# The eight value products of a pair of heads, recorded as one unbroken alternating run on TensorE

## The chip, the cores and the metric

One core of a Trainium2 chip runs the whole kernel. The metric is the device time of one execution in microseconds; a profile of one execution goes with it. The engines are TensorE (PE in the views; PEld for its weight loads), VectorE (DVE), ScalarE (ACT), GpSimd (POOL) and SyncE (SP), which issues most transfers.

## The reference

Two layers of a decoder trunk over 512 positions of width 1024. A layer projects its normed input once, runs three causal token mixers of eight heads of 64 on it, gates each, projects each back, merges and adds. Cut to what matters here:

```python
for l in range(DEPTH):                        # 2 layers
    z = u @ w_in                              # one projection for all mixers
    ya = dsa_attention(...)                   # a: softmax over the top 128 keys of an indexer
    yb = swa_sinks_attention(...)             # b: softmax over a window of 128, with sinks
    yc = stick_breaking_attention(...)        # c: stick-breaking weights, no softmax
    # each of them ends with the value product of every head, for example
    #   einsum('bhts,bshd->bthd', a, v)       # weights (512 x 512, causal) times values (512 x 64)
    merged = sum(sigmoid(m) * ((y * silu(g)) @ w_br) for y, g, m, w_br in ...)
    x = x + gate * (merged @ w_out)
```

## The kernel before

Everything lies transposed: features on the 128 partitions, the 512 positions along the free axis. Weights come from HBM in chunks `wstage` and are split into a high part `whi` and a low part `wlo`; activations are split in the same way (`uh` and `ul`, and both halves of a tile `Y`). A wide projection of one output tile `ps_z` is then 24 matmuls of 512 columns: eight slices of the input with three products each.

A mixer works on pairs of heads, four pairs (0 to 3) each, in the order c, b, a. For a pair, `c_qk` or `softmax_qk` makes the weights in tiles `t` (products `KH,Q` and `klow,Q`), `softmax_tr` transposes them in blocks of 128 on TensorE (`small,t`) and copies them back to tiles `t`, and `softmax_pv` multiplies them with the values `vc`, `vb` or `va`. This last step is the one that changes. The two heads of a pair share one PSUM tile `y` (a `ps_s`): head 0 has partitions 0 to 63, head 1 has 64 to 127. Each head has four products, one for each block j of 128 keys. In mixers a and c they are 512, 384, 256 and 128 columns wide, in mixer b 256, 256, 256 and 128. They are in float32, and each of them leaves two records in the profile. The first product of a head (j is 0) opens its half of the bank, the others add to it. `finish_pair` then multiplies `y` with the gate (`e<-ps_s,G`), and splits it into the two halves of `Y`, which the branch products (`ps_z<-Y,whi` and `ps_z<-Y,wlo`) read.

No operation is issued where it is written. `Weave` first puts the streams of one layer (indexer, top-k search, mixers, projections) into one sequence. Each operation is then recorded by `Recorder.add`, which finds what it depends on, and priced by `Recorder.price`. A list scheduler, `Recorder.forward`, gives every engine its order from these prices and from priorities of earlier rounds, and `Recorder.emit` issues that order. The scheduler may put any other ready TensorE operation between two recorded ones. An operation named `pairs` is an exception: it is recorded once, holds a list of matmuls, and `emit` issues them back to back. Before the change only `low_parts` uses it, for products `klow,Q` of 64 rows. In the views line 553 is where `emit` issues such a list, and line 555 where it issues everything else.

The value products are recorded one by one, the heads in turn for each j:

```python
for j in range(4):
    for e in range(2):
        ...
        mm(y[64 * e:64 * e + 64, 128 * j:128 * j + W], st["v" + b][:, j, c:c + 64], PT[bk][:, c0:c0 + W], j == 0)
```

`price` knows them by their 64 columns of values, and gives each half of the time of its columns and 0.03 us.

Of the kernel before, what the change touches and what calls it, by code (L numbers as in the profile page):

```python
# [25 lines left out]
F32 = mybir.dt.float32  # L26
# [127 lines left out]
class View:  # L154
# [30 lines left out]
    def real(self):  # L185
        ap = self.tile.real()
        for name, arg, *more in self.ops:
            ap = ap.rearrange(arg, a=more[0]) if more else getattr(ap, name)(arg)
        return ap
# [60 lines left out]
class Recorder:  # L250
# [29 lines left out]
    def add(self, ways):  # L280
        x = Instr()
        x.i = len(self.list)
        op, args, kw = next(iter(ways.values()))
        if op == "pairs":
            named = [(("out", "in", "in")[n], v) for q in args for n, v in enumerate(q)]
        else:
            named = [("out" if "out" not in kw and n == 0 else n, v) for n, v in enumerate(args)] + list(kw.items())
        x.writes = [v for n, v in named if isinstance(v, View) and n in ("out", "accum_out")]
        x.reads = [v for n, v in named if isinstance(v, View) and n not in ("out", "accum_out")]
        x.preds, x.succs = {}, []  # L290
        for views, w in ((x.reads, False), (x.writes, True)):
            for v, r in [(v, r) for v in views for r in v.regions()]:
                t = v.tile
                if op == "matmul" and w and kw["start"]:
                    r = (r[0], r[1], 0, S)
                keep = []
                for (j, r2, w2) in t.seen:
                    over = r[0] < r2[1] and r2[0] < r[1] and r[2] < r2[3] and r2[2] < r[3]
                    if over and j is not x and (w or w2):
                        x.preds[j.i] = j  # L300
                    if not (w and over and r[0] <= r2[0] and r2[1] <= r[1] and r[2] <= r2[2] and r2[3] <= r[3] and j is not x):
                        keep.append((j, r2, w2))
                t.seen = keep + [(x, r, w)]
        x.tiles = list({id(v.tile): v.tile for v in x.reads + x.writes if not v.tile.pool.fixed}.values())
        for j in x.preds.values():
            j.succs.append(x)
        x.alts = {}
        for e, (op, args, kw) in ways.items():
            x.alts[e] = self.price(x, e, op, args, kw)
        x.prio = x.i  # L310
        self.list.append(x)

    def price(self, x, engine, op, args, kw):

        y = Way()
        y.op, y.args, y.kw, y.mode, y.port = op, args, kw, None, False
        o = x.writes[0] if x.writes else None
        if op == "preload_act_table_set":
            y.cost = y.lag = 1.3
            return y  # L320
        if op == "dma_start":
            n = 1
            for d in (o or x.reads[0]).shape:
                n *= d
            y.cost, y.lag, y.mode = 0.35 if engine == "SP" else 0.1, n * 4 / 365e3, "dma"
            return y
        n = 1
        for d in o.shape[1:]:
            n *= d
        from_psum = any(v.tile.pool.name[:3] == "ps_" for v in x.reads)  # L330
        if engine == "PE":
            if op == "pairs":
                w = [q[2].shape[-1] for q in args]
                c, y.mode = 0.095 + sum(max(0.112, 0.4375e-3 * v + 0.007) for v in w[::2]), "r"
                y.cost, y.lag = c, c + self.PIPE
            elif op == "transpose":
                c, y.mode = 0.109, "t"
                y.cost, y.lag = c, c + self.PIPE
            elif args[1].shape[-1] == 64:
                c, y.mode = 4 * n / 2.4e3 / 2 + 0.03, "c"  # L340
                y.cost, y.lag = c, 2 * c + self.PIPE
            else:
                rhs, y.mode = args[2], "m"
                c = 4 * n / 2.4e3 + 0.01 if rhs.dtype == F32 else 0.06 if rhs.dtype == BF16 else 0.4375e-3 * n + 0.007
                y.cost, y.lag = c, c + self.PIPE
            return y
        accum = "accum_out" in kw
        if engine == "ACT":
            b = 0.1 if isinstance(kw.get("bias"), View) or isinstance(kw.get("scale"), View) else 0.0
            c = 0.2 + 0.82e-3 * n + (b if not accum else 0.08) - (0.03 if from_psum else 0)  # L350
        elif engine == "DVE":
            y.port = not from_psum and op not in ("max", "match_replace", "memset", "reciprocal")
            if op == "tensor_tensor_scan":
                c = 1.21
            elif op == "max":
                c = 0.15 + 1.05e-3 * args[1].shape[-1]
            elif op == "match_replace":
                c = 0.145 + 1.05e-3 * args[2].shape[-1]
            elif n <= 16:
                c = 0.2 + (0.1 if accum else 0)  # L360
            elif op == "tensor_tensor_reduce":
                c = 0.147 + 1.05e-3 * n
            elif from_psum:
                c = 0.147 + 1.05e-3 * n + (0.08 if accum else 0)
            elif op in ("tensor_scalar", "tensor_copy"):
                c = 0.2 + 0.45e-3 * n if op == "tensor_scalar" else 0.15 + 0.5e-3 * n
            elif op == "memset":
                c = 0.1 + 0.6e-3 * n
            else:
                c = 0.15 + 1.05e-3 * n + (0.08 if accum else 0)  # L370
        else:
            y.port = n > 16
            if op == "memset":
                c = 0.12 if n < 16 else 0.52
            elif op == "tensor_copy":
                c = 0.2 + 0.82e-3 * n
            elif op == "tensor_scalar":
                c = 0.2 + 2.8e-3 * n
            else:
                c = 0.1 + 2.35e-3 * n  # L380
        y.cost = y.lag = c
        return y
# [162 lines left out]
    def emit(self, order):  # L545
        def real(v):
            return v.real() if isinstance(v, View) else v
        with self.tc.manual_schedule():
            for x, engine in order:
                y = x.alts[engine]  # L550
                if y.op == "pairs":
                    for q in y.args:
                        self.real[engine].matmul(*[real(a) for a in q], start=False, stop=True, skip_group_check=True)  # L553
                    continue
                getattr(self.real[engine], y.op)(*[real(a) for a in y.args], **{k: real(v) for k, v in y.kw.items()})  # L555

# [21 lines left out]
def trunk(ctx, tc, xT, vecs, w_ss, w_gt, w_first, w_t, w_v, w_br, w_o, rope, consts, out):  # L578
# [18 lines left out]
    def ybank():  # L597
        return rec.tile("ps_s", [P, S])
# [4 lines left out]
    def mm(o, lhsT, rhs, start, stop=True):  # L603
        PE.matmul(o, lhsT, rhs, start=start, stop=stop, skip_group_check=True)

    def pairs(quads):

        rec.add({"PE": ("pairs", tuple(quads), {})})
# [94 lines left out]
    st = {}  # L703
# [333 lines left out]
    def hold_topk(y):  # L1037

        POOL.tensor_copy(out=m8_tile()[:, 0:1], in_=f(y[:, 0:1]))
# [33 lines left out]
    def low_parts(q, kl, pos, banks, b, order):  # L1073

        quads = []
        for e, i in order:
            k0, W = keys(b, i)
            bk, c0 = pos(e, i)
            hp = (H0, H1)[e]
            quads.append((banks[bk][:, c0:c0 + W], q[hp, e, 128 * i:128 * i + 128], kl[hp, k0:k0 + W]))  # L1080
        pairs(quads)

    LOW_ALL = ((0, 3), (1, 3), (0, 2), (1, 2), (0, 1), (1, 0), (0, 0))
# [62 lines left out]
    def keys(b, i):  # L1146
        return (0, 128 * (i + 1)) if b != "b" else (max(0, 128 * (i - 1)), 256 if i else 128)
# [96 lines left out]
    def softmax_pv(b, p):  # L1244
        def fn():
            y = ybank()
            PT = st.pop(("pt", p))
            tpos = btpos if b == "b" else cpos
            for j in range(4):
                W = min(256, S - 128 * j) if b == "b" else S - 128 * j  # L1250
                for e in range(2):
                    bk, c0 = tpos(e, j)
                    h = 2 * p + e
                    c = 64 * (h // 4 if b == "b" else h)
                    mm(y[64 * e:64 * e + 64, 128 * j:128 * j + W], st["v" + b][:, j, c:c + 64], PT[bk][:, c0:c0 + W], j == 0)
            finish_pair(b, p, y)
            if b == "c":
                hold_topk(st["yc", p][0])
        return op(1500 if b == "b" else 2200, fn)
# [275 lines left out]
    for fn, chunks in wv.items:  # L1535
# [4 lines left out]
        args = [ch.get(pos - len(chunks) + i) for i in range(len(chunks))]  # L1540
# [65 lines left out]
```

## Time and profile before

| | |
|---|---|
| time, median of 3 runs | 1219.87 us (1219.51 to 1220.11) |
| profiled execution, first to last instruction | 1217.8 us; the page gives no other time of its own for it |
| TensorE busy | 1200.4 us (99%), 6006 records |
| VectorE busy | 962.1 us (79%) |
| ScalarE busy | 556.3 us (46%) |
| GpSimd busy | 264.3 us (22%) |
| moved by DMA | 139.40 MB, mean 114 GB/s |

A record of a matmul starts where the matmul starts; its end is modelled and lies under the next one. The time between the starts of two neighbours is therefore what a matmul takes of TensorE. The granted clock of TensorE is 0.998 of full speed over the span. Nearly all instructions carry the line of `emit`, so groups are told apart by the names of their tiles.

### The profile page before, as it was taken

The numbers are of one execution on the slowest core, as the hardware profiler recorded it, in microseconds if no ns is written. First come the engines' busy times: TensorE is split into PE (matmuls) and PEld (weight loads), VectorE is DVE, ScalarE is ACT, GpSimd is POOL, SyncE is SP. The second block draws the span as 40 slices with busy tenths as digits, with TensorE's granted clock in tenths as the row PEclk, the third lists the DMA queues.
The fourth block names the chain that finished last, engine by engine and source line by source line (L and its number), as shares of the span: only waits on it lengthen the run. The fifth ranks groups of instructions, "written<-read, shape, count | busy, mean of one in ns | idle before, by whom it ended". The sixth has DMA issues, their size and how long they took to land.

```text
span 1217.8 us, 17816 instructions
## 1 busy us (share of the span) xinstructions
PE 1200.4 (99%) x6006; PEld 976.3 (80%) x6006; DVE 962.1 (79%) x2106; ACT 556.3 (46%) x1166; POOL 264.3 (22%) x290
## 2 busy tenths in 40 slices
PE   9999999999999999999999999999999999999997
PEld 8899777788777887688898987777878878877886
DVE  6867999899879888686476699989996887667754
ACT  6623677454445532632143157664534654234222
POOL 1200446432111110011200015454220110100120
PEclk9999999999999999999999999999999999999999
DMA  9644222344334455245533432223442324323343
GB/s 318 231 119 124 83 70 84 104 114 117 109 96 122 129 146 150 69 130 145 171 109 98 133 95 78 85 69 116 121 122 70 96 80 120 95 64 79 93 123 102
DMA packets 81915, 139.40 MB, mean 114 GB/s; under 512 B 10016, under 2 KB 22560, under 8 KB 81824
## 3 DMA queue, kind: packets, MB, share of 16 engines
q1 hardware_dynamic: 80672, 136.17, 38.6%
q10 hardware_dynamic: 1152, 2.10, 0.5%
q8 instruction: 47, 0.77, 0.3%
q14 instruction: 44, 0.36, 0.1%
HBM read 125.39 MB, written 4.19 MB: 106 GB/s over the span
## 4 chain that ended last, share of the span: by engine, by line
PE 89%; DVE 4%; SPq 2%; DMA 2%; ACT 1%; issue 1%; POOL 1%; DVEq 0%; ACTq 0%; POOLq 0%
PE ps_z L555 67%; PE ps_s L555 22%; SPq L555 2%; PE ps_s L553 1%; DMA m<-zs 1%; DVE t L555 1%; DVE Q L555 1%; DVE m L555 1%; DMA wstage<-in_w_first 1%; DMA wstage<-in_w_t 0%; ACT t L555 0%; POOL KH L555 0%; DVE score L555 0%; DVE zc L555 0%; DVE den L555 0%
## 5 line engine op out<-in xcount | busy, mean ns | idle before, releaser
L555 PE MATMUL ps_z<-uh,whi 128*128 128x512 f32 (+1 forms) x908 | 359.1, 397 | 2.2 <-DVE xm L555 2.2
L555 PE MATMUL ps_z<-uh,wlo 128*128 128x512 f32 (+1 forms) x908 | 356.0, 393 | 0.0
L555 PE MATMUL ps_z<-ul,whi 128*128 128x512 f32 (+1 forms) x908 | 355.8, 392 | 0.0
L555 POOL TENSOR_TENSOR wlo<-wstage,whi 128x512 fp32r<-128x512 f32 (+1 forms) x131 | 175.1, 1339 | 662.8 <-DVE whi L555 312.0
L555 PEld LDWEIGHTS ps_z<-uh,whi 128*128 128x128 f32 x908 | 170.3, 188 | 41.9 <-DVE xm L555 3.1
L555 PEld LDWEIGHTS ps_z<-uh,wlo 128*128 128x128 f32 x908 | 170.5, 188 | 38.7 <-issue 1.8
L555 PEld LDWEIGHTS ps_z<-ul,whi 128*128 128x128 f32 x908 | 170.6, 188 | 35.9 <-issue 1.0
L555 DVE TENSOR_TENSOR wlo<-wstage,whi 128x512 fp32r<-128x512 f32 (+2 forms) x241 | 158.2, 660 | 12.8 <-ACT whi L555 3.6
L555 DVE CAST whi<-wstage 128x512 fp32r<-128x512 f32 (+2 forms) x181 | 74.7, 412 | 112.9 <-PE ps_z L555 94.5
L555 ACT CAST whi<-wstage 128x512 fp32r<-128x512 f32 (+2 forms) x141 | 83.4, 596 | 169.7 <-PE ps_z L555 125.9
L555 PE MATMUL ps_z<-Y,whi 128*128 128x512 f32 x384 | 121.7, 396 | 0.0
L555 ACT ACTIVATE e<-ps_z 128x512 f32<-128x512 f32 x68 | 40.2, 592 | 131.7 <-PE ps_z L555 131.4
L555 PEld LDWEIGHTS ps_z<-Y,whi 128*128 128x128 f32 x384 | 71.7, 188 | 17.0
L555 ACT ACTIVATE e<-e 128x512 f32<-128x512 f32 x96 | 60.6, 633 | 39.9 <-DVE e L555 39.1
L555 PE MATMUL ps_z<-Y,wlo 128*128 128x512 f32 x192 | 75.8, 395 | 0.0
L555 ACT ACTIVATE t<-t 128x512 f32<-128x512 f32 x120 | 71.8, 628 | 6.1 <-DVE t L555 2.7
L555 ACT ACTIVATE t<-t,nm 128x256 f32<-128x256 f32 (+3 forms) x128 | 65.2, 511 | 18.0 <-DVE nm L555 17.9
L555 PEld LDWEIGHTS ps_s<-small,t 128*128 128x128 f32 x432 | 50.3, 140 | 13.3 <-ACT t L555 2.9
L555 PE MATMUL ps_s<-small,t 128*128 128x128 f32 x432 | 58.6, 274 | 1.8 <-ACT t L555 1.3
L555 POOL CAST whi<-wstage 128x512 fp32r<-128x512 f32 (+2 forms) x50 | 31.2, 623 | 134.0 <-PE ps_z L555 63.1
L555 DVE SCALAR_TENSOR_TENSOR wstage<-wstage,csr 128x512 f32<-128x512 f32 x64 | 47.3, 740 | 9.4 <-DMA wstage<-in_w_ss 6.7
L555 DVE MAX8 m<-score 128x8 f32<-128x256 f32 (+2 forms) x96 | 53.2, 555 | 1.0
(208 smaller groups left out, 2066.8 us busy)
## 6 DMA issues: line engine op xcount, KB each, us to landing
wstage<-in_w_t SPq DMA_DIRECT2D x212, 256.0 KB, 2.7
wstage<-in_w_v SPq DMA_DIRECT2D x48, 182.0 KB, 2.4
Y<-in_w_ss SPq DMA_DIRECT2D x16, 512.0 KB, 6.7
m<-zs SPq DMA_DIRECT2D x128, 64.0 KB, 2.0
wstage<-in_w_gt SPq DMA_DIRECT2D x32, 256.0 KB, 2.7
wstage<-in_w_ss SPq DMA_DIRECT2D x32, 256.0 KB, 2.7
wstage<-in_w_o SPq DMA_DIRECT2D x32, 256.0 KB, 2.7
wstage<-in_w_first SPq DMA_DIRECT2D x16, 256.0 KB, 3.1
```

What stands on the lines that cost most here:

```text
L553: self.real[engine].matmul(*[real(a) for a in q], start=False, stop=True, skip_group_check=True)
L555: getattr(self.real[engine], y.op)(*[real(a) for a in y.args], **{k: real(v) for k, v in y.kw.items()})
```

## The change

`softmax_pv` collects its eight products in a list, in the same order as before (block by block, the two heads in turn), and records them as one `pairs` operation. Each entry of such a list now says whether it opens its part of the bank, so that `add` marks the region and `emit` sets the flag. `price` gives the list the time of one head's columns and 0.03 us, and the price of single products of 64 columns is gone.

```diff
@@ Recorder.add
         if op == "pairs":
-            named = [(("out", "in", "in")[n], v) for q in args for n, v in enumerate(q)]
+            named = [(("out", "in", "in")[n], v) for q in args for n, v in enumerate(q[:3])]
+            opened = {id(q[0]) for q in args if q[3]}
...
-                if op == "matmul" and w and kw["start"]:
+                if w and (op == "matmul" and kw["start"] or op == "pairs" and id(v) in opened):
                     r = (r[0], r[1], 0, S)
@@ Recorder.price
             if op == "pairs":
                 w = [q[2].shape[-1] for q in args]
-                c, y.mode = 0.095 + sum(max(0.112, 0.4375e-3 * v + 0.007) for v in w[::2]), "r"
+                if args[0][2].dtype == F32:
+                    c, y.mode = 0.03 + sum(4 * v / 2.4e3 for v in w[::2]), "c"
+                else:
+                    c, y.mode = 0.095 + sum(max(0.112, 0.4375e-3 * v + 0.007) for v in w[::2]), "r"
                 y.cost, y.lag = c, c + self.PIPE
...
-            elif args[1].shape[-1] == 64:
-                c, y.mode = 4 * n / 2.4e3 / 2 + 0.03, "c"
-                y.cost, y.lag = c, 2 * c + self.PIPE
@@ Recorder.emit
-                        self.real[engine].matmul(*[real(a) for a in q], start=False, stop=True, skip_group_check=True)
+                        self.real[engine].matmul(*[real(a) for a in q[:3]], start=q[3], stop=True, skip_group_check=True)
@@ low_parts
-            quads.append((banks[bk][:, c0:c0 + W], q[hp, e, 128 * i:128 * i + 128], kl[hp, k0:k0 + W]))
+            quads.append((banks[bk][:, c0:c0 + W], q[hp, e, 128 * i:128 * i + 128], kl[hp, k0:k0 + W], False))
@@ softmax_pv
+            quads = []
             for j in range(4):
                 ...
                 for e in range(2):
                     ...
-                    mm(y[64 * e:64 * e + 64, 128 * j:128 * j + W], st["v" + b][:, j, c:c + 64], PT[bk][:, c0:c0 + W], j == 0)
+                    quads.append((y[64 * e:64 * e + 64, 128 * j:128 * j + W], st["v" + b][:, j, c:c + 64], PT[bk][:, c0:c0 + W], j == 0))
+            pairs(quads)
             finish_pair(b, p, y)
```

What this does to the order shows best in two places. The first is TensorE at pair 3 of mixer c in layer 0. Before, the scheduler has put four products of one head first, and wide matmuls between the rest:

```order
L555 MATMUL ps_s<-t,vc 64x512
L555 MATMUL ps_s<-t,vc 64x384
L555 MATMUL ps_s<-t,vc 64x256
L555 MATMUL ps_s<-t,vc 64x128
L555 MATMUL ps_z<-ul_503,whi 128x512
L555 MATMUL ps_s<-t,vc 64x512
L555 MATMUL ps_s<-t,vc 64x384
L555 MATMUL ps_s<-t,vc 64x256
L555 MATMUL ps_z<-uh_468,wlo 128x512
L555 MATMUL ps_z<-uh_522,whi 128x512
L555 MATMUL ps_z<-ul_549,whi 128x512
L555 MATMUL ps_s<-t,vc 64x128
```

Now the eight stand together, x2 being the two heads, and the first products of mixer b follow one wide matmul later (the lines are one or two higher since the file has grown):

```order
L556 MATMUL ps_z<-uh_405,whi 128x512
L556 MATMUL ps_z<-ul_425,whi 128x512
L554 MATMUL ps_s<-t,vc 64x512 x2
L554 MATMUL ps_s<-t,vc 64x384 x2
L554 MATMUL ps_s<-t,vc 64x256 x2
L554 MATMUL ps_s<-t,vc 64x128 x2
L556 MATMUL ps_z<-uh_405,wlo 128x512
L556 MATMUL ps_s<-KH,Q 128x256 x12
```

Three pieces have become one, and it stands behind 13 more wide matmuls. In the whole program the value products stand in 38 pieces before and in 24 afterwards, one for each pair. In 12 of the 24 pairs the heads do not alternate throughout before; these are pairs 0 and 3 of c, 2 and 3 of b, and 2 and 3 of a, in both layers.

The second place is TensorE behind the last pair of mixer a in layer 0, with the numbers of the buffers. `Y_5459` holds the result of that pair. Before, seven wide matmuls come between its last product and its first reader:

```order
L555 MATMUL ps_s_5411<-t_5441,va_1046 64x128
L555 MATMUL ps_z_5436<-uh0_203,wlo_5350 128x512
L555 MATMUL ps_z_5436<-uh1_278,whi_5339 128x512
L555 MATMUL ps_z_5436<-ul1_293,whi_5339 128x512
L555 MATMUL ps_z_5436<-uh1_278,wlo_5350 128x512
L555 MATMUL ps_z_5436<-uh2_373,whi_5339 128x512
L555 MATMUL ps_z_5436<-ul2_396,whi_5339 128x512
L555 MATMUL ps_z_5436<-uh2_373,wlo_5350 128x512
L555 MATMUL ps_z_5224<-Y_5459,whi_5088 128x512
```

Now the result is `Y_5490`, and four come between:

```order
L554 MATMUL ps_s_5470<-t_5461,va_1047 64x128
L556 MATMUL ps_z_5382<-uh7_611,wlo_5373 128x512
L556 MATMUL ps_z_5492<-Y_4248,whi_5426 128x512 x2
L556 MATMUL ps_z_5492<-Y_4248,wlo_5449 128x512
L556 MATMUL ps_z_5219<-Y_5490,whi_5085 128x512
```

The last tile of the projections is already finished there, so three of the four are branch products of an earlier pair. In layer 1 six wide matmuls stand in that place.

## The prediction

> **What bounds the kernel now.** I read the page's engine shares first, then the chain that ended last, then what TensorE waited for, then the stretches in which VectorE has little room, and last, for the change, the stretches with the value products alone.
>
> ```profile
> span 1217.8 us, 17816 instructions
> ...
> PE 1200.4 (99%) x6006; PEld 976.3 (80%) x6006; DVE 962.1 (79%) x2106; ACT 556.3 (46%) x1166; POOL 264.3 (22%) x290
> ...
> PE 89%; DVE 4%; SPq 2%; DMA 2%; ACT 1%; issue 1%; POOL 1%; DVEq 0%; ACTq 0%; POOLq 0%
> ```
>
> TensorE is busy for 1200.4 of 1217.8 us and carries 89% of the chain. A busy share can hide slow matmuls, so it does not yet say that time taken off TensorE comes off the end. What TensorE waited for says that; these are the first, fourth and last of nine rows (us in total, times, longest):
>
> ```profile
> PE ps_z L555 <- DVE xm L555: 2.2, 2, 1.2
> ...
> PE ps_s L555 <- ACT t L555: 1.5, 3, 0.9
> ...
> PE ps_s L555 <- DVE vc L555: 0.2, 1, 0.2
> ```
>
> The largest is 2.2 us and each of the others 1.5 or less, so all nine stay under 15 us in the whole span. Almost everywhere TensorE goes from one matmul straight to the next. A microsecond less work there moves everything behind it forward, unless another engine has no room to follow. VectorE is the nearest to that, in the two stretches in which mixer c of the first layer and the start of mixer b stand:
>
> ```profile
> 108.00:224.00 116.00, 116.00 (x600) 89.37 (x599) 108.86 (x205) 78.06 (x141) 54.40 (x75) 1.00 0.28 80
> ...
> 224.00:250.00 26.00, 24.79 (x123) 19.68 (x123) 22.92 (x63) 13.30 (x36) 10.88 (x9) 1.00 0.39 112
> ```
>
> The columns are the length of the stretch, then the busy time of TensorE, of its weight loads, VectorE, ScalarE and GpSimd, and the granted clock (1.00). In the first, TensorE is full and VectorE has 116.00 - 108.86 = 7.1 us of room.
>
> **What the value products take now.** This is the timeline of TensorE: start, duration, count. First pair 1 of mixer c, whose two heads already alternate, then pair 3, where they do not:
>
> ```profile
> 167.45 0.39 PE L555 MATMUL ps_z<-ul,whi 128*128 128x512 f32 x1
> 167.68 0.40 PE L555 MATMUL ps_z<-uh,wlo 128*128 128x512 f32 x1
> 168.00 2.37 PE L555 MATMUL ps_s<-t,vc 128*64 128x512 f32 x16
> 170.31 0.50 PE L555 MATMUL ps_z<-uh,whi 128*128 128x512 f32 x1
> 170.64 0.39 PE L555 MATMUL ps_z<-ul,whi 128*128 128x512 f32 x1
> ...
> 217.48 2.37 PE L555 MATMUL ps_s<-t,vc 128*64 128x512 f32 x8
> 219.78 0.50 PE L555 MATMUL ps_z<-ul,whi 128*128 128x512 f32 x1
> 220.20 2.15 PE L555 MATMUL ps_s<-t,vc 128*64 128x512 f32 x6
> 222.28 0.50 PE L555 MATMUL ps_z<-uh,wlo 128*128 128x512 f32 x1
> ...
> 223.18 0.43 PE L555 MATMUL ps_s<-t,vc 128*64 128x128 f32 x2
> 223.54 0.50 PE L555 MATMUL ps_z<-uh,wlo 128*128 128x512 f32 x1
> ```
>
> Each float32 product leaves two records, so x16 is the eight products of a pair. Alternating, all eight take 170.31 - 168.00 = 2.31 us. In pair 3, four products of one head take 219.78 - 217.48 = 2.30 us alone, the next three 2.08 and the last 0.36. So the second head is free when it alternates with the first, and costs its full time when the scheduler lets one head go first. The recorded 2.37 holds some 0.06 us that lie under the next matmul.
>
> The same timeline prices the edge of a piece. Two wide matmuls stand 0.23 us apart (167.45 to 167.68), the last one ahead of the products 0.32 (to 168.00), and the first one behind 0.33 (170.31 to 170.64). So each separate piece of value products costs another 0.09 + 0.10 = 0.19 us beside its own time.
>
> All of them, from the stretches with only these products counted (length, TensorE busy with its records in brackets, then the weight loads). In order: mixer c with pair 0, pairs 1 and 2, pair 3, for each layer; mixer b with pairs 0 and 1, pairs 2 and 3; mixer a likewise:
>
> ```profile
> 140.00:150.00 10.00, 3.28 (x16) 1.75 (x16) 0.00 (x0) 0.00 (x0) 1.00 0.25 80
> 160.00:200.00 40.00, 4.75 (x32) 2.12 (x32) 0.00 (x0) 0.00 (x0) 1.00 0.29 87
> 215.00:226.00 11.00, 4.95 (x16) 1.94 (x16) 0.00 (x0) 0.00 (x0) 1.00 0.28 75
> 735.00:745.00 10.00, 3.28 (x16) 1.75 (x16) 0.00 (x0) 0.00 (x0) 1.00 0.31 79
> 760.00:795.00 35.00, 4.75 (x32) 2.12 (x32) 0.00 (x0) 0.00 (x0) 1.00 0.30 84
> 812.00:822.00 10.00, 4.95 (x16) 1.94 (x16) 0.00 (x0) 0.00 (x0) 1.00 0.22 68
> ...
> 245.00:320.00 75.00, 3.55 (x32) 2.63 (x32) 0.00 (x0) 0.00 (x0) 1.00 0.43 116
> 330.00:365.00 35.00, 7.12 (x32) 3.97 (x32) 0.00 (x0) 0.00 (x0) 1.00 0.33 98
> 840.00:915.00 75.00, 3.56 (x32) 2.65 (x32) 0.00 (x0) 0.00 (x0) 1.00 0.41 116
> 925.00:960.00 35.00, 5.71 (x32) 3.72 (x32) 0.00 (x0) 0.00 (x0) 1.00 0.28 78
> ...
> 385.00:480.00 95.00, 4.75 (x32) 2.12 (x32) 0.00 (x0) 0.00 (x0) 1.00 0.49 142
> 490.00:520.00 30.00, 8.38 (x32) 3.18 (x32) 0.00 (x0) 0.00 (x0) 1.00 0.26 77
> 980.00:1072.00 92.00, 4.75 (x32) 2.12 (x32) 0.00 (x0) 0.00 (x0) 1.00 0.35 98
> 1085.00:1115.00 30.00, 8.39 (x32) 3.31 (x32) 0.00 (x0) 0.00 (x0) 1.00 0.19 50
> ```
>
> Where two pairs take 4.75 (mixers a and c) or 3.55 us (mixer b), they already alternate. Of the 24 pairs, twelve do not: pairs 0 and 3 of c, 2 and 3 of b, 2 and 3 of a, in each layer.
>
> **The change, part by part.**
>
> 1. The products themselves. Now the fourteen rows add up to 25.96 (c) + 19.94 (b) + 26.27 (a) = 72.17 us. Afterwards every pair has the order of those that alternate now: 16 pairs of a and c at 4.75 / 2 = 2.375, 8 of b at 3.55 / 2 = 1.775, together 38.0 + 14.2 = 52.2 us. Difference 20.0 us. Before, the order has these products in 38 pieces, afterwards in 24, and 0.06 us of each piece lies under the next matmul: 14 x 0.06 = 0.8 us of the difference is not on the path. That leaves 19.1 us. The price of the new form is taken from the same instructions in the same order, so I see no other end for it.
>
> 2. Fewer pieces. 14 fewer edges at 0.19 us are 2.7 us. On TensorE together 19.1 + 2.7 = 21.8 us, all of it in stretches where it is full.
>
> 3. The block waits for all of its operands. Before, the first head could start when its transposed copies were there; now TensorE takes the pair later and does other matmuls first. Pair 3 of c in layer 0 stands behind 13 more wide matmuls. The wait for a copy is at worst one ScalarE copy:
>
> ```profile
> L555 ACT COPY t<-ps_s 128x512 f32<-128x512 f32 x73 | 40.1, 589 | 11.4 <-PE ps_s L555 11.1
> ```
>
> It is 589 ns. In front of the last pair of mixer a in layer 0 the new order has six wide matmuls between the last transposes and the block, 6 x 0.23 = 1.4 us, which cover it; so I cost this at nothing. Without that cover it would be up to 0.6 us a pair, 14 us over 24.
>
> 4. What reads the block. Behind the last pair of a in layer 0, the fill has run out: the new order has four wide matmuls, then the branch product that needs this pair. The finish on VectorE shows its length in that place:
>
> ```profile
> 517.29 0.50 PE L555 MATMUL ps_z<-uh,wlo 128*128 128x512 f32 x1
> ...
> 517.40 0.69 DVE L555 TENSOR_TENSOR e<-ps_s,G 128x512 f32<-128x512 f32 x1 [2.18 <-PE ps_s L555]
> 518.12 0.43 DVE L555 CAST Y<-e 128x512 fp32r<-128x512 f32 x1
> ```
>
> The cast ends at 518.12 + 0.43 = 518.55, so 1.26 us after the block; four wide matmuls cover 0.33 + 3 x 0.23 = 1.02. A new wait of some 0.3 us once. In layer 1 six of them stand there and cover it (1.5 us).
>
> 5. Everything else. The scheduler has new costs for the products and lays all engines anew, but no instruction is added or taken away, and the weight loads from HBM keep their sequence among themselves. What could be lost is room on VectorE. In mixer c TensorE loses 0.9 (pair 0) + 2.6 (pair 3), less 0.1 for the tails, plus 0.4 for two edges = 3.7 us per layer; VectorE's room there shrinks from 7.1 to 3.4 us and it would be 97% busy. If none of that could be used, 2 x 3.7 = 7.4 us would come back as waits; if the new layout also closed the waits that are there, a microsecond or two would be gained. Because VectorE still has room, and part of its work there is the top-k search, which is needed only in mixer a, I stay near the low end and take 0.8 us, an estimate.
>
> Sum: 21.8 - 0.3 - 0.8 = 20.7 us. The span goes from 1217.8 to 1197.1 us. The median of the runs shown, 1219.87 us, lies 2.1 us above the profiled span, and I carry that over: 1199.2 us, 1.7% faster.
>
> One rule of the skill gives another sum. The Trainium skill ("TensorE: Matmul & The Clock Gate", Part 3) tells of 2.38 times for three column tiles, which by proportion (an estimate) is 1.59 for two. One head alone is 2.30 us here, so by it a pair would take 2 x 2.30 / 1.59 = 2.9 us rather than 2.31, and the eight pairs of a and c that change would save 8 x 0.59 = 4.7 us less, about 1204 us. The rows of this case disagree: 2.31 against 2.30 us is a factor of 2.0 for two heads.
>
> **The rivals.**
>
> - VectorE sets the pace in mixer c: the 3.7 us per layer come back whole as waits ahead of the products or their transposes, in place of my 0.8. Then 1199.2 + 7.4 - 0.8 = 1205.8 us. For it: 108.86 of 116.00 us busy there, and 22.92 of 26.00 behind. Against it: 7.1 us of room.
> - The heads overlap only in part. Pair 0 of mixer c shows that: its heads are mixed in groups of three products, and it takes 3.28 us, not 2.375. If a pair that is new in this order came out like it, the eight pairs of a and c would cost 8 x 0.9 = 7.2 us more: 1206.4 us. Against it: in pairs 1 and 2 the heads alternate product by product, as all will, and two pairs take 4.75. The page named above would put this case near its 1204.
> - Slower: the block is too large a piece, and TensorE stands in front of each until two copies in a row have come, 2 x 0.59 us with no other matmul to fill in. It decides when 24 blocks wait 21.8 / 24 = 0.9 us on average; at the full 1.18 us it is 24 x 1.18 = 28.3 us, so 1219.87 - 21.8 + 28.3 = 1226.4 us. Against it: pairs that go as one piece now (168.00) have no idle time in front.
> - No effect: the pieces that are saved lie beside a chain on other engines. For it: the chain has 11% off TensorE. Against it: TensorE's waits for others are under 15 us in all, and 20 us cannot vanish beside a chain that has that little slack. Time about 1219 us.
>
> **How the numbers follow.** My forecast (1196.5 to 1202 us) has a chance of 0.70; VectorE in mixer c 0.17; part overlap 0.05; no effect 0.03; slower 0.02; and 0.03 for a layout that also closes old waits, below 1196.5. The range from 1195 to 1206 us takes in the forecast, the low case and nearly all of VectorE's. A change of about 0.2% is what a measurement here can tell from none: faster by more 0.95, within it 0.03, slower 0.02.
>
> **What would show it.** In the profile after: the stretches with the products alone add up to 52 us in place of 72, each pair in one piece at 2.37 or 1.73 to 1.78 us; TensorE busy for about 1180 us; waits of TensorE still near 10 us, with one new of about 0.3 us for the result of the last pair of a in layer 0. I am wrong if TensorE's waits for VectorE or ScalarE grow by several microseconds in mixer c or at the start of b, or if blocks take 3 us.

## Result, and the profile after

The changed kernel takes 1205.4 us (median of four, 1204.95 to 1206.9) against 1219.99 us (1219.51 to 1220.51) of the kernel before beside it: ratio 0.9884 (95% interval 0.9871 to 0.9897), 14.6 us less. The forecast was 1199.2 us. The direction held, and so did the range from 1195 to 1206 us, by 0.6 us. The band from 1196.5 to 1202 us, which had a chance of 0.70, was missed: some 6 us of the gain that it counted on did not arrive.

The head of the page after, with the engine shares and the chain that ended last:

```profile
span 1203.5 us, 17819 instructions
...
PE 1181.2 (98%) x6006; PEld 969.7 (81%) x6006; DVE 958.3 (80%) x2094; ACT 565.8 (47%) x1177; POOL 257.3 (21%) x291
...
PE 86%; DVE 6%; DMA 3%; ACT 2%; SPq 2%; issue 1%; POOL 0%; DVEq 0%; ACTq 0%
```

TensorE's busy time fell by 1200.4 - 1181.2 = 19.2 us, the span by only 1217.8 - 1203.5 = 14.3. VectorE's share of the chain rose from 4% to 6%. VectorE has 12 instructions less, ScalarE 11 more and GpSimd one more: an operation that may run on one of two engines is placed by the scheduler, and some have changed places.

What TensorE waited for after the change, the first four, the seventh and the eighth of eleven rows (us in total, times, longest). Line 556 is now where `emit` issues single operations, 554 where it issues lists:

```profile
PE ps_s L556 <- DVE t L556: 5.8, 4, 3.0
PE ps_z L556 <- ACT e L556: 2.3, 2, 1.2
PE ps_s L556 <- DVE wlo L556: 1.3, 2, 1.0
PE ps_s L556 <- DVE m L556: 1.2, 1, 1.2
...
PE ps_z L556 <- DVE xm L556: 0.9, 2, 0.5
PE ps_z L556 <- ACT uh L556: 0.7, 1, 0.7
```

All eleven add up to 15.1 us; before, nine rows made 10.1. The wait for VectorE's `t` is now 5.8; this was its row before:

```profile
PE ps_s L555 <- DVE t L555: 0.5, 2, 0.3
```

The one for `xm`, then the largest with 2.2, has shrunk to 0.9.

The stretches with the value products alone, one or two of them for each mixer, in the columns of the prediction (c pairs 0, 1 and 2, 3 of layer 0; then b pairs 0 and 1, 2 and 3; then a likewise):

```profile
140.00:150.00 10.00, 2.38 (x16) 1.06 (x16) 0.00 (x0) 0.00 (x0) 1.00 0.26 94
165.00:200.00 35.00, 4.75 (x32) 2.12 (x32) 0.00 (x0) 0.00 (x0) 1.00 0.29 83
220.00:230.00 10.00, 2.37 (x16) 1.06 (x16) 0.00 (x0) 0.00 (x0) 1.00 0.45 124
...
240.00:320.00 80.00, 3.47 (x32) 2.12 (x32) 0.00 (x0) 0.00 (x0) 1.00 0.42 123
325.00:362.00 37.00, 3.47 (x32) 2.12 (x32) 0.00 (x0) 0.00 (x0) 1.00 0.34 102
...
375.00:475.00 100.00, 4.75 (x32) 2.23 (x32) 0.00 (x0) 0.00 (x0) 1.00 0.48 139
485.00:520.00 35.00, 4.75 (x32) 2.13 (x32) 0.00 (x0) 0.00 (x0) 1.00 0.26 74
```

Every pair of a and c takes 2.375 us and every pair of b 1.735, in both layers; all fourteen stretches make 51.9 us against 72.17 before. So the products did what was forecast, and the missing time lies elsewhere.

To find it I took, for each matmul in the two traces, the time from its start to the next one's start, and as its usual step the median of that for the same kind of matmul with the same kinds of neighbours. What lies above the usual step is waiting or slow clock. Summed over the span:

| us | before | after | difference |
|---|---|---|---|
| value products, start to start | 69.5 | 50.2 | -19.3 |
| edges of the pieces (38, then 24) | | | about -2.5 |
| above the usual step | 13.5 | 21.1 | +7.5 |
| sum | | | -14.3 |

The sum is the difference of the two spans. The two figures in the third row depend on what is called usual. Their difference does not: it is what the other rows leave of the 14.3 us. The 7.5 us stand in a few places. This is TensorE's timeline at the largest, the transposes of pair 3 of mixer c in layer 1, and VectorE and GpSimd in the same microseconds (start, duration, then the idle time in front and who ended it in brackets):

```profile
799.12 0.39 PE L556 MATMUL ps_z<-uh,whi 128*128 128x512 f32 x1
802.49 0.66 PE L556 MATMUL ps_s<-small,t 128*128 128x128 f32 x2 [2.98 <-DVE t L556]
802.80 0.78 PE L556 MATMUL ps_z<-ul,whi 128*128 128x512 f32 x1
803.37 0.63 PE L556 MATMUL ps_z<-uh,wlo 128*128 128x512 f32 x1
```

```profile
796.81 4.28 DVE L556 TENSOR_TENSOR KH<-zc,KH 64x512 fp32r<-64x512 f32 x3
801.12 1.22 DVE L556 TENSOR_TENSOR_SCAN t<-ps_s,t 128x511 f32<-128x511 f32 x1
```

```profile
796.57 1.28 POOL L556 TENSOR_TENSOR wlo<-wstage,whi 128x512 fp32r<-128x512 f32 x1
...
797.86 1.28 POOL L556 TENSOR_TENSOR wlo<-wstage,whi 128x512 fp32r<-128x512 f32 x1
```

A wide matmul should be followed after 0.23 us; here it takes 802.49 - 799.12 = 3.37. The transposes need a scan of mixer c, and on VectorE three subtractions for mixer b's keys (`KH<-zc,KH`) stand ahead of it for 4.28 us. In the single records the first of them takes 2.88 us and the others 0.69 and 0.70: it began while GpSimd was at a `wlo`, and ended 0.55 us after the second `wlo` (797.86 + 1.28 = 799.14). The Trainium skill ("SBUF — State Buffer", Who interferes with whom) says that a VectorE instruction with two SBUF inputs and a GpSimd instruction that reads SBUF shut each other out; these rows agree, with 2.88 against 0.69 us. Before the change the four key subtractions stood on GpSimd, and no row of TensorE's waits named them:

```profile
803.89 2.67 POOL L555 TENSOR_TENSOR KH<-zc,KH 64x512 fp32r<-64x512 f32 x2
...
806.80 2.64 POOL L555 TENSOR_TENSOR KH<-zc,KH 64x512 fp32r<-64x512 f32 x2
```

The same three subtractions stand there in layer 0 (4.04 us, and 1.5 us of wait). The other new waits are in mixer a:

```profile
486.60 0.40 PE L556 MATMUL ps_z<-Y,wlo 128*128 128x512 f32 x1
488.36 0.50 PE L556 MATMUL ps_s<-KH,Q 128*128 128x512 f32 x1 [1.36 <-DVE t L556]
...
512.65 0.49 PE L556 MATMUL ps_z<-uh,wlo 128*128 128x512 f32 x1
514.26 0.70 PE L556 MATMUL ps_z<-Y,whi 128*128 128x512 f32 x2 [1.11 <-ACT e L556]
...
1092.81 0.50 PE L556 MATMUL ps_z<-uh,whi 128*128 128x512 f32 x1 [1.18 <-ACT e L556]
```

Start to start, less the usual step, the list of places is (us):

| place | after less before |
|---|---|
| c, pair 3, transposes, layer 0 (215.36) and layer 1 (802.49) | +1.5 and +2.6 |
| slow clock behind 802.49 (below) | +1.5 |
| a, pair 2, layer 0 (488.36) | +1.5 |
| a, behind the last pair, layer 0 (514.26) | +1.3 |
| a, layer 1 (1092.81) | +1.1 |
| start of b, wait for `xm`, both layers | -1.3 |
| b, layer 0 (354.18 before) | -1.1 |

Together 7.1 of the 7.5 us.

### The profile page after: what moved, and what is told of

It is laid out like the page before. It is cut to its first block, busy times and chain, and to the rows that moved or that the text cites. A ratio compares the mean times of both kernels' runs of the same rounds, so it can differ in the third digit from the quotient of the medians.

```text
span 1203.5 us, 17819 instructions
## 1 busy us (share of the span) xinstructions
PE 1181.2 (98%) x6006; PEld 969.7 (81%) x6006; DVE 958.3 (80%) x2094; ACT 565.8 (47%) x1177; POOL 257.3 (21%) x291
## 4 chain that ended last, share of the span: by engine, by line
PE 86%; DVE 6%; DMA 3%; ACT 2%; SPq 2%; issue 1%; POOL 0%; DVEq 0%; ACTq 0%
PE ps_z L556 67%; PE ps_s L556 14%; PE ps_s L554 5%; DMA wstage<-in_w_first 2%; DVE t L556 2%; SPq L556 2%; ACT t L556 1%; DVE KH L556 1%; DMA m<-zs 1%; DVE m L556 0%; DVE Y L556 0%; DVE zc L556 0%; DVE Q L556 0%; DVE wlo L556 0%; DMA wstage<-in_w_ss 0%
## 5 line engine op out<-in xcount | busy, mean ns | idle before, releaser
L556 POOL TENSOR_TENSOR wlo<-wstage,whi 128x512 fp32r<-128x512 f32 (+1 forms) x131 | 172.6, 1318 | 623.3 <-DVE whi L556 302.1
L556 DVE TENSOR_TENSOR wlo<-wstage,whi 128x512 fp32r<-128x512 f32 (+2 forms) x241 | 159.0, 663 | 14.3 <-ACT whi L556 4.9
L556 ACT CAST whi<-wstage 128x512 fp32r<-128x512 f32 (+2 forms) x149 | 88.5, 597 | 169.1 <-PE ps_z L556 128.6
L556 DVE CAST whi<-wstage 128x512 fp32r<-128x512 f32 (+2 forms) x171 | 71.0, 416 | 112.9 <-PE ps_z L556 96.2
L556 POOL CAST whi<-wstage 128x512 fp32r<-128x512 f32 (+2 forms) x52 | 33.8, 651 | 200.8 <-PE ps_z L556 135.2
L556 PEld LDWEIGHTS ps_s<-small,t 128*128 128x128 f32 x432 | 51.1, 142 | 14.2 <-issue 5.8
L556 PE MATMUL ps_s<-KH,Q 128*128 128x256 f32 (+3 forms) x280 | 52.0, 309 | 1.4 <-DVE t L556 1.4
```

## Experiments

Two theories for the 6 us that were lost. **A, the layout**: the new prices made the scheduler lay out VectorE and GpSimd in another way, with the key subtractions ahead of the scans; the old layout would have kept the gain. **B, the pace**: whatever the layout, a TensorE that arrives earlier finds VectorE, and what it waits for itself, not yet there, and the waits return in one place or another. Each run was compared with the kernel before on the same chip (1219.52, 1219.79 and 1220.09 us in the three groups).

### e1: the old order on all engines, the eight products gathered

The kernel before, with its order kept; only the value products of a pair are taken out and put, alternating, at the place of the last of them.

```diff
-        return best[1]
+        return self.gather(best[1])
+    def gather(self, order):
+        ...                       # last[k], group[k]: by output tile
+            elif last[id(x.writes[0].tile)] == n:
+                out += [(v, "PE") for v in sorted(group[id(x.writes[0].tile)], key=lambda v: v.i)]
```

> The order of the kernel before on every engine, except that the pieces of each pair's value products are gathered, alternating, at the place of the last piece. Both theories: the products take 50.2 us, 24 pieces, so 21.9 us less on TensorE. Theory A (the new layout made the new waits: it puts three subtractions KH<-zc,KH of mixer b's keys on VectorE ahead of the last scans of pair 3 of c): the old layout has them on GpSimd, TensorE's waits stay near the 10 us of before, time 1198 to 1200 us. Theory B (the waits come with any faster TensorE, because the chains on VectorE and ScalarE were covered by its lateness): waits grow by 5 to 8 us here too, 1203 to 1206 us.

Measured: 1207.88 us (1207.87 to 1209.05), ratio 0.9906 (0.9891 to 0.9921), span 1206.1. It lies above both expected ranges, since the products did not come down to 50.2 us (below). By the table above: products -15.1, edges about -2.5, above the usual step +5.9. The first rows of TensorE's waits here and in the changed kernel differ in name and agree in size:

```profile
PE ps_z L573 <- DVE xm L573: 4.2, 2, 2.4
```

`xm`, at the start of mixer b, waits for VectorE, which is still in line there: in pair 3 of c TensorE's block of products ended 2.5 us earlier than before (221.03 for 223.54), VectorE's reading of it only 0.5 us (224.02 for 224.54). So with the order of the other engines untouched 5.9 us come back as well, some 1.5 of them slow clock behind the longest wait. That speaks for B; A alone would have left the waits as they were.

This run also shows a cost that the changed kernel does not have. Each product waits for its own operand, and where one waits in the middle of a pair, the heads fall out of step: in pair 3 a copy of `t` on VectorE ends at 219.54, and the product that needs it starts at 219.59, 0.65 us behind its partner of the other head. Pair 0 and pair 3 of c in layer 0, 2.38 and 2.37 us in the changed kernel:

```profile
140.00:150.00 10.00, 2.83 (x16) 1.62 (x16) 0.00 (x0) 0.00 (x0) 1.00 0.31 81
...
212.00:226.00 14.00, 3.07 (x16) 1.43 (x16) 0.00 (x0) 0.00 (x0) 1.00 0.28 79
```

Hence 54.4 us for the products (start to start) instead of 50.2. A list is no protection against this. `emit` issues its products one behind the other, each with its own waits; in the changed kernel the copies were simply there in time. Among the other prices below are three blocks in which they were not.

### e2: the changed kernel with the heads in turn

The same layout and the same list, issued as four products of head 0, then four of head 1.

```diff
-                    for q in y.args:
+                    for q in (y.args[0::2] + y.args[1::2] if y.mode == "c" else y.args):
```

> The changed kernel's order and blocks, but within a block all products of one head come first, then those of the other. From the rows of before a pair costs 2.30 + 2.08 us or so in a and c and 2 x 1.66 in b: 16 x 4.4 + 8 x 3.3 = 96.8 us in place of 50.2, so 46.6 us more. Theory A (layout): the waits in front of the transposes of pair 3 of c stay, 1250 to 1253 us. Theory B (cover): 2 us more of TensorE per pair cover them, waits fall back to 10 us, 1244 to 1247 us.

Measured: 1236.69 us (1235.23 to 1237.39), ratio 1.0138 (1.0123 to 1.0153), 31 us above the changed kernel. One pair of a, and two pairs of b:

```profile
385.00:395.00 10.00, 3.93 (x16) 1.81 (x16) 0.00 (x0) 0.00 (x0) 1.00 0.37 119
...
245.00:325.00 80.00, 5.30 (x32) 3.46 (x32) 0.00 (x0) 0.00 (x0) 1.00 0.40 121
```

Start to start a pair of a or c takes 3.86 us against 2.31, of b 2.58, 82.3 us in all. Both expected ranges lay higher, as they took a pair at the time of two heads alone, 4.4 us or so. It is less, since the second head's first products run beside the first head's last: in the pair of a above, the second head starts at 391.79 us, while the first head begins its third product at 391.78. So the order within the list is worth more than the whole change; that the eight products stand together is not enough.

The waits stayed where they were, in size too:

```profile
PE ps_s L556 <- DVE t L556: 5.7, 4, 3.0
```

B in the simple form that slower blocks would cover these waits falls: the transposes of pair 3 of c wait as long as in the changed kernel although TensorE has spent more time on the blocks ahead. VectorE's order is the same there, with the three subtractions ahead of the scan, and that was not moved by slower blocks.

### e3: the key subtractions fixed on GpSimd

```diff
-                both(kl[a, kv], r[a], f(kh[a, kv]), OP.subtract)
-                both(kl[b, kv], r[a], f(kh[a, kv]), OP.subtract)
+                POOL.tensor_tensor(out=kl[a, kv], in0=r[a], in1=f(kh[a, kv]), op=OP.subtract)
+                POOL.tensor_tensor(out=kl[b, kv], in0=r[a], in1=f(kh[a, kv]), op=OP.subtract)
```

> The changed kernel, with the four subtractions KH<-zc,KH of mixer b's keys allowed on GpSimd alone (in the kernel before they ran there). Theory A: the waits of 1.5 us (layer 0) and 3.0 us (layer 1) in front of pair 3's transposes go, 1200.5 to 1202 us. Theory B: another VectorE or ScalarE chain is late in the same place, less than 1.5 us gained, 1204 to 1206 us.

Measured: 1202.14 us (1201.48 to 1203.3), ratio 0.9857 (0.9843 to 0.9872), span 1200.1, 3.3 us under the changed kernel by medians. The subtractions are back on GpSimd, and the waits have moved:

```profile
791.93 4.02 POOL L556 TENSOR_TENSOR KH<-zc,KH 64x512 fp32r<-64x512 f32 x3
```

```profile
PE ps_z L556 <- DVE xm L556: 2.8, 2, 1.8
PE ps_s L556 <- DVE t L556: 2.3, 4, 1.4
```

In front of pair 3's transposes 0.4 and 0.8 us are left; the wait for `xm`, 0.9 after the change, has grown to 2.8. Time above the usual step: 17.8 us against 21.1. So at this price A holds for about 3.3 us, net of what came back one stage later, as B says. The scheduler laid out everything else anew as well; what the trace shows of the keys themselves is that the waits in front of pair 3 shrank.

### e4, e5, e6, e7, e9: other prices for the block

If the layout is worth microseconds, the price that produces it should be as well. The constant 0.03 in the block's price was set to 0.17 (e4), 0.10 (e9), and with e3's edit to 0.17 (e5), 0.10 (e6) and 0.25 (e7):

```diff
-                    c, y.mode = 0.03 + sum(4 * v / 2.4e3 for v in w[::2]), "c"
+                    c, y.mode = 0.10 + sum(4 * v / 2.4e3 for v in w[::2]), "c"
```

> The changed kernel with 0.17 in place of 0.03 us in the price of a block, which makes it what a block takes on the chip (2.30 and 1.66 us). The products and their order within a block are the same. If the waits came because blocks were priced 0.14 us too low, the layout now fits and waits fall to 10 us: 1199 to 1201 us. If they come from VectorE's and ScalarE's work (both A and B), the price of a block does nothing for them but moves the layout by chance: 1199 to 1209 us, with the waits in other places.

> Both edits at once: mixer b's key subtractions on GpSimd alone, and 0.17 us in the price of a block. Each alone gave about 3 us. If they take away waits in different places, they add up: 1199 to 1200.5 us. If both only move the same waits in pair 3 of c, or the layout is chance, 1201 to 1205 us.

> The same with 0.10 us in the price. If the price matters through its nearness to the chip, this lies between 0.03 (1202.1 us) and 0.17. If layouts differ by chance, it may lie anywhere from 1198 to 1206 us, also outside of the two.

> The same with 0.25 us, 0.08 more than a block takes. By nearness it is no better than 0.17; by chance 1198 to 1206 us. The products take 50.2 us in all three, so that any difference beyond 1 us is TensorE's waits.

> The changed kernel with 0.10 in place of 0.03 us in the price of a block, the key subtractions free as in the changed kernel. The best so far has this price and the keys on GpSimd (1201.1 us). If the keys matter in this layout too, VectorE has them ahead of pair 3's scans again and it takes 1203 to 1206 us; if it was chance where they fell, 1200 to 1203 us. The products take 50.2 to 51 us either way.

| | keys | price | us, median (lowest to highest) | ratio (interval) | largest wait of TensorE |
|---|---|---|---|---|---|
| changed kernel | free | 0.03 | 1205.4 (1204.95 to 1206.9) | 0.9884 (0.9871 to 0.9897) | DVE t 5.8 |
| e9 | free | 0.10 | 1207.85 (1206.17 to 1208.88) | 0.99 (0.9883 to 0.9917) | ACT t 2.6 |
| e4 | free | 0.17 | 1202.79 (1200.61 to 1203.66) | 0.9864 (0.9848 to 0.988) | ACT t 2.5 |
| e3 | GpSimd | 0.03 | 1202.14 (1201.48 to 1203.3) | 0.9857 (0.9843 to 0.9872) | DVE xm 2.8 |
| e6 | GpSimd | 0.10 | 1201.09 (1199.68 to 1204.21) | 0.9851 (0.9835 to 0.9867) | DVE t 2.0 |
| e5 | GpSimd | 0.17 | 1206.68 (1204.18 to 1209.65) | 0.9902 (0.9885 to 0.9918) | DVE xm 5.1 |
| e7 | GpSimd | 0.25 | 1202.82 (1202.36 to 1203.21) | 0.9862 (0.9847 to 0.9876) | ACT t 3.4 |

The products take 50.2 to 51.1 us in all seven; the times differ by 6.8 us, nearly all of it through the layout. The 0.9 us among the products are one block, the first pair of mixer a in layer 0, which waits for copies in its middle in e4, e5 and e7; here it is in e5:

```profile
375.00:390.00 15.00, 3.13 (x16) 1.60 (x16) 0.00 (x0) 0.00 (x0) 1.00 0.46 138
```

Nothing adds up: e3's edit gains 3.3 us at 0.03, 6.8 at 0.10, and loses 3.9 at 0.17. Nor does the time follow the price: e4 missed the range for a price that fits (1199 to 1201 us), e5 and e9 came out above both of their ranges, and e6 below both of its neighbours. Where the keys stand does not settle it either: e4 has two of the four subtractions on VectorE, ahead of the last scan of pair 3, and takes as long as e3, which has none there. The largest wait has another name in nearly every row; here are the first rows of the lists of e6 and e5:

```profile
PE ps_s L556 <- DVE t L556: 2.0, 1, 2.0
PE ps_z L556 <- ACT e L556: 2.0, 2, 1.2
```

```profile
PE ps_z L556 <- DVE xm L556: 5.1, 2, 3.0
```

e6 has the lowest median, and its ratio's interval lies below that of the changed kernel; it beats both kernels, and cannot be told from e3, e4 and e7. It is a good layout among several that were tried, not a better price.

### e8: e1 with one weight load moved ahead

In e1 the wait for `xm` begins with VectorE standing at a cast whose chunk has not come, as SyncE issues four small transfers (`m<-zs`) ahead of its load. e8 is e1 with one load a layer issued ahead of the four.

```diff
-        return self.gather(best[1])
+        return self.earlier(self.gather(best[1]))   # on SyncE: wstage<-in_w_t, then four m<-zs
```

> The old order with gathered products (1207.9 us), with one change per layer: behind pair 3 of c, the weight chunk that SyncE issues behind four small transfers m<-zs goes ahead of them. If the waits of TensorE for xm there (1.9 us in layer 0, 2.6 us in layer 1) come from that chunk, which VectorE's next cast waits for with everything behind it, the cast comes up to 2.4 us earlier and the waits fall below 1 us each: 1204.5 to 1206.5 us. If VectorE is simply full there, or the four transfers become what is late, they stay: 1207 to 1209 us.

VectorE in layer 0, first e1, then e8:

```profile
230.07 0.43 DVE L573 CAST whi<-wstage 128x512 fp32r<-128x512 f32 x1 [0.90 <-DMA wstage<-in_w_t]
```

```profile
228.58 0.69 DVE L595 TENSOR_TENSOR m<-m,rt 128x512 f32<-128x512 f32 x1 [1.17 <-DMA m<-zs]
229.19 0.42 DVE L595 CAST whi<-wstage 128x512 fp32r<-128x512 f32 x1
```

Measured: 1206.83 us (1206.63 to 1207.37), ratio 0.9894 (0.9879 to 0.9909), 1.05 us under e1. The wait for `xm` fell from 1.9 to 0.8 us in layer 0 and from 2.6 to 2.5 in layer 1. The cast no longer waits, but what stands ahead of it now waits 1.17 us for one of the four transfers. The wait was handed from one transfer to the next; about a microsecond of it was the order of the issues. The time falls between the two expected ranges, and the intervals of e1 and e8 overlap, so the microsecond rests on the trace of layer 0 more than on the times.

## Why the prediction was right or wrong

1. **The products**: right. 19.1 us were forecast for the path, 19.3 measured; a pair takes 2.31 us start to start, as priced from pair 1. Pairs of b came out at 1.735 for 1.775, since pair 0 of b is no longer the slower one. The rival of a partial overlap, 0.05, did not come in the changed kernel, and the proportion from the Trainium skill ("TensorE: Matmul & The Clock Gate", Part 3), about 2.9 us a pair, is not borne out: it is 2.31. Out-of-step pairs like it do exist, in e1 (2.83, 3.07) and in e4, e5 and e7 (3.00 to 3.25), and there it was a wait within the pair that caused them.

2. **Fewer pieces**: right, 2.7 forecast and about 2.5 measured.

3. **The block waits for all operands**: right in its cost, not in its mechanism. No wait of TensorE stands in front of a block or in it, so the term was nothing, as forecast. But only the scheduler treats a block as waiting once; on TensorE each product waits for its own copy, as single ones do, and where a copy comes late the block falls out of step, by 0.6 to 0.9 us in e4, e5 and e7.

4. **Behind the last pair of a, layer 0**: the right place, the wrong wait. 0.3 us were forecast because `Y` would be late. It is 1.3 us, and the list names ScalarE's `e<-ps_z`, which must empty an output tile before a new one can use it. I had followed the operand and not the output slot (the kernel has three tiles `ps_z`). The operand would not have been ready either: its cast to `Y`, on ScalarE now, ended at 514.63, 1.98 us after the block instead of 1.26.

5. **Everything else**: the step that failed, by its size. I allowed 0.8 us for lost room, with a bound of 7.4. Measured is 7.5 less the 1.3 of step 4, so 6.2 us. By the steps: 21.8 - 1.3 - 6.2 = 14.3 us. Two things were wrong in it. The search for lost room was confined to mixer c, where about 4 us came (waits of 4.1 in front of pair 3, 1.5 of slow clock, less 1.3 at `xm`). Another 2.6 came in mixer a, less 1.1 in b. And "no instruction is added or taken away" was taken to mean that the other engines carry the same work, while three key subtractions changed from GpSimd to VectorE.

The sign of being wrong that the prediction named did come: TensorE's wait for VectorE in mixer c grew by several microseconds. The first rival gave 1205.8 us, and the time is 1205.4. That they agree so closely is luck, and with it that the range held, since its mechanism is only half of what happened: VectorE is the engine waited for in c, but with the keys on GpSimd 3.3 us of the loss went, so at this price that much hangs on the layout and not on VectorE's amount of work, and mixer a was not in it at all. The share that stays with any layout cannot be separated cleanly. But the changed kernel, e1 and e3 to e7 had 15.2 (e4) to 21.1 us above the usual step, and none of them as little as the 13.5 of before; e9 had more, as its span is 2.3 us longer than the changed kernel's with the same products. So some loss came with every layout, 1.7 us in the best (whose profiled run, 1200.61 us, was the fastest of its four) and 5.9 in the one that kept the old order. One wait came back in all of them: the one for ScalarE's `e`, 1.1 to 2.3 us in the changed kernel and in each of the nine runs, and in no row of the kernel before. Why a given layout lands where it does is open; a schedule without these waits was not tried. The rivals of no effect and of a slower kernel did not come; TensorE's short list of waits had spoken against both.

## What to carry to other kernels

Price a new form of the work from rows in which it already exists: the term of 19.1 us came out within 0.2. Then ask where the faster engine will arrive earlier, in every stage and not only the fullest, and look there at three things: the neighbour's queue, who owns the output slot, and which operations the scheduler may put on another engine. Here that was worth 2 to 10 us, not one, and where a scheduler lays the kernel out, measure a few of its prices before judging the change: seven layouts of the same work spread over 6.8 us here, nearly half of the gain of 14.6.

## What the runs showed of the hardware

**A wait of 2.3 to 3 us can halve TensorE's clock, and it matters where it falls.** Two consecutive stretches of the changed kernel around the wait that ends at 802.49 (length, busy times of the five engines, then the granted clock in the third column from the end):

```profile
798.92:802.33 3.41, 0.59 (x3) 0.16 (x1) 3.35 (x5) 0.61 (x2) 0.22 (x1) 1.00 0.50 175
802.33:805.74 3.41, 3.25 (x11) 2.78 (x12) 3.34 (x5) 1.26 (x2) 2.29 (x4) 0.50 0.00 0
```

The clock is 0.50 for these 3.41 us, so the wait costs about 1.5 us more than it shows. In e1 the same happened a microsecond behind its longest wait (2.40 us listed, 2.6 us start to start above the step):

```profile
828.00:830.00 2.00, 2.00 (x6) 1.61 (x5) 1.97 (x5) 2.00 (x11) 0.60 (x1) 0.50 0.22 48
```

There wide matmuls stand 0.43 us apart instead of 0.23. The length of a wait does not decide it alone. A wait of 2.30 us in e8 halved the clock as well; one of 2.38 us in e9, which ends at 238.03, did not, and two short ones of e9, 0.74 and 1.06 us with few matmuls between them, did:

```profile
236.79:240.20 3.41, 2.17 (x10) 1.81 (x11) 3.38 (x11) 3.41 (x16) 0.71 (x1) 1.00 0.24 78
240.20:243.61 3.41, 3.41 (x16) 2.75 (x15) 3.38 (x12) 2.43 (x5) 0.91 (x1) 1.00 0.00 0
503.03:506.44 3.41, 1.60 (x12) 1.15 (x11) 2.85 (x9) 3.41 (x12) 0.00 (x0) 1.00 0.55 154
506.44:509.85 3.41, 3.41 (x13) 3.13 (x14) 1.48 (x4) 2.14 (x5) 0.00 (x0) 0.50 0.00 0
```

In every trace the changes of the clock lie whole multiples of 3.413 us apart (233 of them, 795.3 us, from the first change in the changed kernel to the one at 802.33). If the eleven spans are cut on that grid, the cases separate: once the clock is full, all 18 stretches in which TensorE's records fill 1.61 us or less are followed by half clock, and none is in which they fill 1.70 us or more. The grid begins at another place in each execution (the first change is at 7.02 us in the changed kernel and at 4.55 us in e1), so one and the same wait may cost the clock in one execution and not in another. The Trainium skill ("TensorE: Matmul & The Clock Gate", Part 1) gives half clock after an idle window of about 3.4 us. The length agrees with these traces; that the window must be idle throughout does not, as 0.59 us of work in the changed kernel and 1.60 us in e9 were not enough to keep the clock.

**Two heads on one array are free only in step.** The same eight products took 2.31 us when they alternate without a wait, 2.8 to 3.2 with a wait among them, and 3.86 with the heads in turn.
